# A GLA and convolution trunk on one core: v and output gate projected together, 512 columns wide, weights in three assigned places, layer 0's output projection block by block

## The chip, the cores and the metric

The kernel runs on one core of a Trainium2 chip. The metric is the device time of one execution, in microseconds; the time before is the median of three runs.

## What is computed

The input is 2048 tokens of 1024 channels in float32. Two residual layers follow each other, each ahead of its mixer with an RMSNorm, and a last RMSNorm ends it. The first layer (the kernel calls it layer 0) is gated linear attention with four heads; the second (layer 1) is a convolution module with a causal depthwise convolution of 31 taps, a layernorm and two gates. The change lies in the first:

```
proj = h @ w_in                      # q, k (512 each), v, z (1024 each), g_lr (16)
log_a = log_sigmoid(g_lr @ w_g2 + b_g) / 16
# per head (dk 128, dv 256), in chunks of 64 tokens:
b = cumsum(log_a);  q_dec = q*exp(b);  k_inv = k*exp(-b);  k_end = k*exp(b_last - b)
o = tril(q_dec @ k_inv.T) @ v + q_dec @ S;   S = exp(b_last)*S + k_end.T @ v
o = rmsnorm_per_head(o) * gn_w * silu(z)
x = x + o @ w_out
```

## The kernel before

Precision: every projection runs as three float32r matmuls, since each operand is split into a high part (`ah`, `wh`) and a low part (`al`, `wl`): high x high, high x low, low x high (`mm3`).

Weights: they come from HBM in units of 128 x 2048 values (1 MB). `load_unit` brings a unit in two halves through the staging tile `wr` (two of them); ScalarE casts each half to `wh`, GpSimd subtracts to get `wl` (VectorE for the first two units). Two places hold units; a place is free when TensorE's last matmul with it is done. `next_unit` keeps two units ahead, in the order of the list `order`.

Layer 0 works on half the tokens at a time (1024, two blocks of 512). `start_block` loads x, splits it (`prep_x`) and computes the low-rank gate (`gate_low`: sixteen matmuls with the gate weights `wgs`, a tile of its own) and E = exp(b). Then `head` runs four times: `qk` projects q and k feature-major, 128 columns of the weights against 512 tokens; `values` projects v for eight tiles of 128 tokens, token-major, 24 matmuls of 256 columns each; a loop over the same eight tiles then projects the gate z, again 24 matmuls of 256 columns, and issues the attention core in three stages, one tile apart: `scores`, `mix` and `turn`. v stays in eight pairs of tiles meanwhile. `out1` is the output projection: pairs of weight units, each pair against block 0 and then block 1. Its sum of squares for the next layer is added on GpSimd. After block 0 of the second pair it calls `ahead`, which prepares the next half's (or layer 1's) first block.

Layer 1 projects, convolves on VectorE, ScalarE and GpSimd beside it, normalises, and projects out. A scheduler places the instructions on each engine's in-order queue from a model of their times and from priorities; SP's queue issues all DMAs, also in order. PSUM has three banks `mm` for projections, two `pb` and three `pm`.

## Time and profile before

| what | us |
|---|---|
| median of the runs (1691.0 to 1695.15) | 1691.66 |
| span of the profiled execution | 1691.3 |
| TensorE busy in it | 1617.2 (96%) |
| VectorE busy | 1015.6 (60%) |
| GpSimd busy | 936.0 (55%) |
| ScalarE busy | 742.2 (44%) |
| layer 0, first half of the tokens | about 0 to 457 |
| layer 0, second half | about 457 to 858 |
| layer 1 | about 858 to 1691 |

Busy times are those of one profiled execution. Matmuls are pipelined, so a matmul's row is longer than the step from its start to the next one's; the steps are what adds up to time.

### The profile page before, as it was taken

Reading aid. Unit: us, or ns where it says so; the run is one execution under the profiler, and the core shown is the slowest. Engines: PE = TensorE matmul, PEld = TensorE weight load, DVE = VectorE, ACT = ScalarE, POOL = GpSimd, SP = SyncE. Lnnn points to the kernel's source line nnn. Section 1 sums busy time; section 2 is a strip of 40 time slices with the busy share of each in tenths; the row PEclk is TensorE's granted clock in tenths of the full one; section 3 lists DMA queues with packets and bytes.
Section 4 is the critical chain, followed back from the end, with each engine's and each line's share of the span. In section 5 each row is a group of like instructions: output and inputs, shape, how many; then the busy total and the mean of one; then the engine's idle time right before and its main releaser. Section 6 shows DMA issues by size and latency. Waiting matters only on the chain.

```text
span 1691.3 us, 23564 instructions
## 1 busy us (share of the span) xinstructions
PE 1617.2 (96%) x9028; PEld 1413.4 (84%) x9028; DVE 1015.6 (60%) x1473; ACT 742.2 (44%) x1254; POOL 936.0 (55%) x795
## 2 busy tenths in 40 slices
PE   8999999999999999999999999998999999997887
PEld 6989998988889999999888887876777778776687
DVE  7423232342334323226153999989799999987865
ACT  6645252343466444325232544544462554434432
POOL 4444343334745342424433999983788997465553
PEclk9999999999999999999999999999999999998998
DMA  5021111244511121204461111225127122632743
GB/s 188 30 78 57 63 51 57 76 130 139 164 34 55 58 72 42 75 33 132 132 196 46 63 50 57 85 80 154 38 69 238 61 68 94 206 125 88 235 176 124
DMA packets 74015, 165.68 MB, mean 98 GB/s; under 512 B 7760, under 2 KB 16464, under 8 KB 73904
## 3 DMA queue, kind: packets, MB, share of 16 engines
q1 hardware_dynamic: 73904, 164.19, 29.9%
q8 instruction: 70, 1.15, 0.3%
q14 instruction: 41, 0.34, 0.1%
HBM read 128.51 MB, written 35.65 MB: 97 GB/s over the span
## 4 chain that ended last, share of the span: by engine, by line
PE 62%; DVE 16%; POOL 7%; DMA 6%; issue 4%; ACT 3%; SPq 0%; POOLq 0%; DVEq 0%; ACTq 0%
PE mm L144 52%; DVE pb L638 6%; PE pb L144 3%; DVE al L190 2%; DMA wr<-in_wall_dram 2%; PE pb L388 1%; POOL wl L125 1%; PE pb L390 1%; POOL convB L624 1%; DVE S L713 1%; PE pm L379 1%; POOL convA L624 1%; DVE d L734 1%; POOL b L736 1%; DVE pb L642 1%
## 5 line engine op out<-in xcount | busy, mean ns | idle before, releaser
L144 PE MATMUL mm<-ah,wh 128*128 128x512 f32 (+1 forms) x1600 | 599.1, 389 | 43.2 <-DVE u L761 10.7
L144 PE MATMUL mm<-al,wh 128*128 128x512 f32 (+1 forms) x1600 | 594.6, 387 | 1.7 <-DVE al L190 1.7
L144 PE MATMUL mm<-ah,wl 128*128 128x512 f32 (+1 forms) x1600 | 592.9, 387 | 2.3 <-POOL wl L125 2.3
L125 POOL TENSOR_TENSOR wl<-wr,wh 128x1024 fp32r<-128x1024 f32 x140 | 358.5, 2575 | 195.2 <-ACT wh L124 190.3
L144 PEld LDWEIGHTS mm<-ah,wh 128*128 128x128 f32 x1600 | 304.0, 191 | 109.0 <-DVE u L761 13.1
L144 PEld LDWEIGHTS mm<-ah,wl 128*128 128x128 f32 x1600 | 303.3, 191 | 62.4 <-POOL wl L125 4.2
L144 PEld LDWEIGHTS mm<-al,wh 128*128 128x128 f32 x1600 | 303.9, 191 | 59.7 <-DVE al L190 2.6
L144 PE MATMUL mm<-wh,ah 128*128 128x256 f32 x896 | 259.2, 289 | 0.0
L144 PE MATMUL mm<-wh,al 128*128 128x256 f32 x896 | 254.6, 284 | 0.0
L144 PE MATMUL mm<-wl,ah 128*128 128x256 f32 x896 | 254.2, 284 | 0.0
L124 ACT ACTIVATE wh<-wr 128x1024 fp32r<-128x1024 f32 x144 | 145.3, 1050 | 109.0 <-PE mm L144 78.9
L638 DVE SCALAR_TENSOR_TENSOR pb<-u,C,pb 128x512 f32<-128x512 f32 x252 | 183.8, 747 | 0.5
L638 DVE SCALAR_TENSOR_TENSOR pb<-u,dwc,pb 128x512 f32<-128x512 f32 x240 | 179.4, 748 | 1.6
L144 PEld LDWEIGHTS mm<-wl,ah 128*128 128x128 f32 x896 | 171.4, 191 | 0.4
L144 PEld LDWEIGHTS mm<-wh,ah 128*128 128x128 f32 x896 | 171.3, 191 | 0.4
L144 PEld LDWEIGHTS mm<-wh,al 128*128 128x128 f32 x896 | 171.3, 191 | 0.0
L622 ACT ACTIVATE prod<-u,C 128x512 f32<-128x512 f32 x148 | 105.6, 721 | 137.6 <-POOL convA L624 78.5
L624 POOL TENSOR_TENSOR convA<-convA,prod 128x512 f32<-128x512 f32 x74 | 99.5, 1344 | 6.6 <-ACT prod L622 3.0
L624 POOL TENSOR_TENSOR convB<-convB,prod 128x512 f32<-128x512 f32 x74 | 99.6, 1346 | 3.9 <-ACT convB L620 0.7
L397 DVE SCALAR_TENSOR_TENSOR S<-S,dec,pb 128x256 f32<-128x256 f32 x56 | 26.8, 479 | 95.4 <-PE pb L144 95.3
L401 POOL TENSOR_TENSOR ss<-ss,e 128x1 f32<-128x1 f32 x64 | 13.3, 208 | 124.5 <-ACT g L400 124.5
L523 DVE TENSOR_TENSOR Q<-mm,Q 128x512 f32<-128x512 f32 x32 | 22.0, 688 | 92.7 <-PE mm L144 78.9
(205 smaller groups left out, 2245.3 us busy)
## 6 DMA issues: line engine op xcount, KB each, us to landing
wr<-in_wall_dram SPq DMA_DIRECT2D x144, 512.0 KB, 4.1
raw<-in_xT_dram SPq DMA_DIRECT2D x32, 256.0 KB, 3.8
Q<-in_xT_dram SPq DMA_DIRECT2D x32, 256.0 KB, 3.2
x_scratch<-Q SPq DMA_DIRECT2D x32, 256.0 KB, 3.2
sz_scratch<-t SPq DMA_DIRECT2D x32, 256.0 KB, 2.3
b<-sz_scratch SPq DMA_DIRECT2D x32, 256.0 KB, 3.8
g_scratch<-st SPq DMA_DIRECT2D x48, 128.0 KB, 1.9
raw<-g_scratch SPq DMA_DIRECT2D x24, 256.0 KB, 3.7
```

The costliest lines, as they stand in the source:

```text
L124: act.activation(wh[:, ks, :], raw, AF.Copy)
L125: (dve if i < 2 else pool).tensor_tensor(wl[:, ks, :], raw, wh[:, ks, :].bitcast(F32), ALU.subtract)
L144: pe.matmul(ps, s, m, start=(i == 0), stop=(i == 3 * n - 1))
L190: dve.tensor_tensor(lo, src, hi.bitcast(F32), ALU.subtract)
L379: pe.matmul(s_ps[:, 0:192], ki[:, js], Q[:, j].rearrange("p s c -> p (s c)"), start=True, stop=True)
L388: pe.matmul(o_ps, Q[:, j, 0:2].rearrange("p s c -> p (s c)"), S[h], start=True, stop=False)
L390: pe.matmul(o_ps, x, y, start=first and n == 0, stop=n == 2)
L397: dve.scalar_tensor_tensor(S[h], S[h], dec[:, j:j + 1], kv, ALU.mult, ALU.add)
L523: dve.tensor_tensor(xr, ps, xr, ALU.add)
L622: act.activation(p, src, AF.Copy, scale=w)
L624: pool.tensor_tensor(acc, acc, p, ALU.add)
L638: dve.scalar_tensor_tensor(dstm, src, w, ps, ALU.mult, ALU.add)
```

## The change

The weights of a head's v and gate are packed side by side, 512 columns wide, and come as two units, each with half of the 1024 input channels. `values` now projects both in 24 matmuls of 512 columns into one bank, takes v from its first half and the gate from its second, and the core's stages run in the same loop. The units have three places, assigned by hand in `order`: place 2 lies in a pool of layer 0 alone. `out1` runs block 0 with all four units and then block 1 with all four, so that its units are loaded twice; `ahead` is called between the blocks. The gate weights lose their own tile: they are built once in a staging tile `wr`, written to HBM, and read back into a `wr` for each of the three later blocks. Head 0 takes block 0's q and k, four token tiles, then starts block 1. `raw` has four buffers where it had five, `vh` and `vl` three where they had eight.

```
-    wp = ctx.enter_context(tc.tile_pool(name="wp", bufs=2))
+    wp = ctx.enter_context(tc.tile_pool(name="wp", bufs=1))
...
-    order = list(range(0, 16)) * 2
+    half = [(3 * h + j, (2, 0, 1)[j]) for h in range(HEADS) for j in range(3)]
+    half[1:3] = [(1, 1), (2, 0)]
+    half += [(12 + j, c) for j, c in enumerate((2, 0, 1, 2))]
+    half += [(12 + j, c) for j, c in enumerate((0, 2, 1, 0))]
+    order = half * 2
+    units = []
     for sched in SCHED:
...
+    order += [(u, (n + 1) % 2) for n, u in enumerate(units)]
...
+        wpool = wq if place == 2 else wp
+        wh = wpool.tile([P, UW], F32R, name=f"wh{place}")
+        wl = wpool.tile([P, UW], F32R, name=f"wl{place}")
...
+    def prefetch(n):
+
+        while len(wstate["ready"]) < n and wstate["next"] < len(order):
+            if order[wstate["next"]][1] in [u[1] for u in wstate["ready"]]:
+                return
+            load_unit()
...
+    def next_wide(expect, ahead):
+
+        prefetch(ahead)
+        w = []
+        for s in range(2):
+            hl = [t.rearrange("p (k c) -> p k c", c=2 * DV) for t in pop_unit(expect + s)]
+            w += [(hl[0][:, k], hl[1][:, k]) for k in range(KT // 2)]
+        return w
...
+    def gate_weights(first):
+
+        t = wp.tile([P, UW // 2], F32R, name="wr", bufs=2)
+        wgs = t.rearrange("p (k c) -> p k c", c=P)
+        if not first:
+            sp.dma_start(out=t.bitcast(F32), in_=wgd)
+            return wgs
...
+    def values(hf, i, w, a_b):
+
+        ps = mm_bank()
+        proj_t(ps, w, a_b, i % 4)
+        q = hf * 8 + i
+        vh, vl = (l1p.tile([P, DV], F32R, name=n, bufs=3) for n in ("vh", "vl"))
+        act.activation(vh, ps[:, 0:DV], AF.Copy, scale=r2[:, q:q + 1])
+        dve.scalar_tensor_tensor(vl, ps[:, 0:DV], r2[:, q:q + 1], vh.bitcast(F32), ALU.mult, ALU.subtract)
+        sz = l1p.tile([P, DV], F32, name="sz", bufs=3)
+        act.activation(sz, ps[:, DV:2 * DV], AF.Silu, scale=rt[:, q:q + 1])
+        return (vh, vl), sz
...
+        w = next_unit(base, 3)
+        if h == 0:
+            qkb.append(qk(h, w, a[0], EEs[0]))
+            wv = next_wide(base + 1, 2)
+            for i in range(4):
+                tokens(i, wv)
+            start_block(hf, 1, a, EEs, g3s)
+            qkb.append(qk(h, w, a[1], EEs[1]))
+            prefetch(1)
+        else:
+            for b in range(2):
+                run_late(1 if b == 0 else 0)
+                qkb.append(qk(h, w, a[b], EEs[b]))
+            wv = next_wide(base + 1, 3)
+            for i in range(4):
+                tokens(i, wv)
+        if h < HEADS - 1:
+            nxt = gate(h + 1, g3s)
+        for i in range(4, 8):
+            tokens(i, wv)
...
-        for pair in range(2):
-            ws = [next_unit(12 + 2 * pair), next_unit(13 + 2 * pair)]
-            for b in range(2):
+        for b in range(2):
+            t0 = hf * TH + b * NB
+            acc = l1p.tile([P, NB], F32, name="acc", bufs=2)
+            for u in range(4):
+                w = next_unit(12 + u, 3)
```

The scheduler's queues show what this does to the order. SP's queue near the program's start; `raw` are tiles of x, `wr` are staging tiles, `wr_126` holds the gate weights. Before:

```order
L123 DMA wr_170<-in_wall_dram 128x1024
L269 DMA raw_176<-in_xT_dram 128x512
L123 DMA wr_201<-in_wall_dram 128x1024 [waits DMAHW0_49]
L247 DMA ident_84<-in_ident_dram 128x128 [waits DMAHW1_49]
L269 DMA raw_185<-in_xT_dram 128x512 [waits DMAHW2_49,DVE_49,Activation_49]
L249 DMA tmp_215<-in_wg2_dram 96x512 [waits DMAHW3_49]
L269 DMA raw_194<-in_xT_dram 128x512 [waits DMAHW4_49,DVE_49,Pool_49]
```

and now:

```order
L133 DMA wr_175<-in_wall_dram 128x1024
L279 DMA wg_scratch_115<-wr_126 128x1024 [waits DVE_49]
L283 DMA ident_84<-in_ident_dram 128x128 [waits DMAHW0_49]
L285 DMA tmp_220<-in_wg2_dram 96x512 [waits DMAHW1_49]
L305 DMA raw_181<-in_xT_dram 128x512 [waits DMAHW2_49,DVE_49,Activation_49]
L286 DMA masks_116<-in_masks_dram 128x192 [waits DMAHW3_49]
L305 DMA raw_190<-in_xT_dram 128x512 [waits DMAHW4_49,DVE_49,Pool_49]
L305 DMA raw_199<-in_xT_dram 128x512 [waits DMAHW5_49,DVE_49,Activation_49]
L305 DMA raw_212<-in_xT_dram 128x512 [waits DMAHW6_49,DVE_49,Pool_49]
L133 DMA wr_206<-in_wall_dram 128x1024 [waits DMAHW7_49,DVE_49]
```

The second half of unit 0 (`wr_201`, now `wr_206`) stood two rows behind the first and now stands nine rows behind it, with a wait for VectorE.

TensorE's queue where the first token tile is projected, behind block 0's q and k. Before, v alone (`wh_275` is its unit; `pm_241` is a sum of squares):

```order
L144 MATMUL pb_365<-wh_275,ah_136 128x256 [waits Activation_49]
L144 MATMUL pb_394<-wh_275,ah_136 128x256
L144 MATMUL pb_365<-wl_276,ah_136 128x256 [waits DVE_49]
L144 MATMUL pb_365<-wh_275,al_137 128x256
L144 MATMUL pb_365<-wh_275,ah_143 128x256
L144 MATMUL pb_365<-wl_276,ah_143 128x256
L144 MATMUL pb_365<-wh_275,al_144 128x256
L166 MATMUL pm_241<-ones_85,acc_135 128x1 [waits DVE_49]
L166 MATMUL pm_241<-ones_85,acc_135 128x1 x3
L144 MATMUL pb_365<-wh_275,ah_152 128x256
```

and now the second half of the channels of v and gate (`wh0_290`, the second unit; `pm_267` is the gate), and the first row of the second token tile:

```order
L172 MATMUL mm_370<-wh0_290,ah_179 128x512 [waits Activation_49]
L172 MATMUL mm_370<-wl0_291,ah_179 128x512 [waits Pool_49]
L172 MATMUL mm_370<-wh0_290,al_180 128x512
L172 MATMUL mm_370<-wh0_290,ah_188 128x512
L172 MATMUL mm_370<-wl0_291,ah_188 128x512
L172 MATMUL mm_370<-wh0_290,al_189 128x512
L346 MATMUL pm_267<-g3_264,g2t_114 128x512 [waits DVE_49,PE_49]
L172 MATMUL mm_370<-wh0_290,ah_197 128x512 [waits Activation_49]
L172 MATMUL mm_370<-wl0_291,ah_197 128x512 [waits Pool_49]
```

Four rows that wait for casts or GpSimd's splits of the second unit now stand inside the first token tile's group.

TensorE's queue in the output projection of the first half, where the next half's sixteen gate matmuls stand. Before, in the last quarter (`mm_4533` is a projection of block 1 with the third unit), ten of the sixteen, each with a wait, and the other six some 40 rows later:

```order
L144 MATMUL mm_4533<-ah_3923,wh_3965 128x512
L166 MATMUL pm_4376<-ones_85,acc_3953 128x1 [waits PE_49,Pool_49]
L288 MATMUL pm_4447<-ah_4384,wgs_111 128x512 [waits Activation_49]
L288 MATMUL pm_4447<-al_4385,wgs_111 128x512 [waits DVE_49]
L288 MATMUL pm_4447<-ah_4391,wgs_111 128x512 [waits Activation_49]
L288 MATMUL pm_4447<-al_4392,wgs_111 128x512 [waits DVE_49]
L288 MATMUL pm_4447<-ah_4399,wgs_111 128x512 [waits Activation_49]
```

and now, in block 1's second unit, with the first nine behind one wait:

```order
L172 MATMUL mm_3676<-ah_3112,wh2_3582 128x512 [waits DVE_49,Activation_49]
L172 MATMUL mm_3676<-al_3113,wh2_3582 128x512
L193 MATMUL pm_3456<-ones_85,acc_3160 128x1 [waits PE_49,Pool_49]
L324 MATMUL pm_3529<-ah_3464,wr_3527 128x512 [waits DMAHW3_49,PE_49]
L324 MATMUL pm_3529<-al_3465,wr_3527 128x512
L324 MATMUL pm_3529<-ah_3471,wr_3527 128x512
L324 MATMUL pm_3529<-al_3472,wr_3527 128x512
L324 MATMUL pm_3529<-ah_3479,wr_3527 128x512
```

The gate matmuls moved from the third and fourth unit's part to the second's, and read their weights from a staging tile that was loaded for them.

## Rows read from the trace of the kernel before

**Rows 1.** The page's parts 1 and 2: busy us per engine; granted clock, 40 slices.
```profile
PE 1617.2 (96%) x9028; PEld 1413.4 (84%) x9028; DVE 1015.6 (60%) x1473; ACT 742.2 (44%) x1254; POOL 936.0 (55%) x795
PEclk9999999999999999999999999999999999998998
```
**Rows 2.** Chain of waits: start us, length us, what; matmuls without a gap, counted.
```profile
144.25 14.39 PE mm L144 x120
...
372.81 56.49 PE mm L144 x249
```
**Rows 3.** Waits of TensorE: us in total, times, longest; layer 0, then layer 1.
```profile
PE pm L310 <- DVE g L302: 1.4, 1, 1.4
PE pb L144 <- DVE vl L438: 1.3, 1, 1.3
...
PE mm L144 <- DVE Q L332: 1.0, 1, 1.0
...
PE mm L144 <- DVE u L761: 10.7, 5, 3.2
PE mm L144 <- DVE u L845: 7.5, 5, 2.3
```
**Rows 4.** Stretches: us, busy us (instructions) of each engine, clock, DMA share, GB/s.
```profile
142.00:225.00 83.00, 83.00 (x591) 78.46 (x591) 24.95 (x52) 34.21 (x70) 30.24 (x40) 1.00 0.18 58
...
372.00:457.00 85.00, 85.00 (x381) 70.51 (x380) 24.86 (x29) 31.04 (x48) 46.61 (x29) 1.00 0.49 150
0.00:27.54 27.54, 19.17 (x65) 14.28 (x66) 21.89 (x28) 19.62 (x31) 9.66 (x21) 1.00 0.80 251
...
858.00:1691.00 833.00, 772.49 (x3540) 638.02 (x3538) 712.29 (x922) 361.20 (x524) 583.81 (x390) 0.97 0.34 112
```
**Rows 5.** Groups by line and form: count, busy us, mean ns, idle before.
```profile
L144 PE MATMUL mm<-wh,ah 128*128 128x256 f32 x896 | 259.2, 289 | 0.0
...
L144 PE MATMUL pb<-wh,ah 128*128 128x256 f32 x128 | 37.4, 294 | 1.3 <-DVE vl L438 1.3
...
L438 DVE SCALAR_TENSOR_TENSOR vl<-mm,r,vh 128x256 fp32r<-128x256 f32 x48 | 22.9, 483 | 89.3 <-ACT vh L437 89.2
...
L437 ACT ACTIVATE vh<-mm,r 128x256 fp32r<-128x256 f32 x48 | 22.1, 469 | 55.2 <-PE mm L144 55.2
...
L318 ACT ACT_TABLE_LOAD x10 | 12.8, 1283 | 0.2
```
**Rows 6.** Timelines of the start: SP (DMA issue), VectorE, TensorE; start us, length us.
```profile
3.55 0.44 SPq L123 DMA_DIRECT2D wr<-in_wall_dram  x1
...
4.50 0.67 SPq L123 DMA_DIRECT2D wr<-in_wall_dram  x1
...
12.50 1.21 DVE L125 TENSOR_TENSOR wl<-wr,wh 128x1024 fp32r<-128x1024 f32 x1
...
25.27 0.39 PE L288 MATMUL pm<-al,wgs 128*128 128x512 f32 x1
...
27.54 0.40 PE L144 MATMUL pb<-wh,ah 128*128 128x256 f32 x2
...
48.43 0.50 PE L144 MATMUL mm<-ah,wh 128*128 128x512 f32 x1 [0.95 <-DVE Q L332]
```
**Rows 7.** What staging costs: landing (whole run; first 60 us), cast (mean ns), GpSimd's splits.
```profile
wr<-in_wall_dram SPq DMA_DIRECT2D x144, 512.0 KB, 4.1
...
wr<-in_wall_dram SPq DMA_DIRECT2D x8, 512.0 KB, 4.8
...
L124 ACT ACTIVATE wh<-wr 128x1024 fp32r<-128x1024 f32 x144 | 145.3, 1050 | 109.0 <-PE mm L144 78.9
...
400.78 4.75 POOL L125 TENSOR_TENSOR wl<-wr,wh 128x1024 fp32r<-128x1024 f32 x2 [3.44 <-ACT wh L124]
```
**Rows 8.** TensorE's timeline where the second half starts, and that stretch's clock (after the busy times).
```profile
469.60 0.39 PE L144 MATMUL mm<-ah,wh 128*128 128x512 f32 x1
471.26 0.39 PE L144 MATMUL pb<-wh,ah 128*128 128x256 f32 x1 [1.27 <-DVE vl L438]
...
472.19 0.28 PE L144 MATMUL pb<-wl,ah 128*128 128x256 f32 x1
473.84 0.47 PE L310 MATMUL pm<-g,g2t 96*128 96x512 f32 x1 [1.37 <-DVE g L302]
...
474.20:481.00 6.80, 6.80 (x34) 6.80 (x33) 1.93 (x5) 6.02 (x7) 3.20 (x3) 0.50 0.00 1
```

More of the change, by code (lines that the diff above doesn't have):

```diff
@@ L103 @@
              U[:3] + Z[:1] + U[3:6] + Z[1:2] + U[6:] + Z[2:]]
[L104 removed]
+    half = [(3 * h + j, (2, 0, 1)[j]) for h in range(HEADS) for j in range(3)]
[4 more added lines that the diff above has]
+    units = []
     for sched in SCHED:
[L106 to L107 removed]
+        units += [16 + j if s == "u" else 24 + j for s, j in sched]
+    units += list(range(28, 32)) * 4
+    order += [(u, (n + 1) % 2) for n, u in enumerate(units)]
     wstate = {"next": 0, "ready": []}
```

120 lines of the change are left out of this document (41 added, 79 removed).

## The prediction

> **What bounds the kernel now.** The page's first part says TensorE is busy 96% of the span, and its granted clock stands at 2.4 GHz in nearly every slice [rows 1]. A busy matmul row proves little, because the matmuls overlap, so the next view is the timeline of starts: from one start to the next is what a matmul really costs. The chain of waits gives the same number in one row, pieces of uninterrupted matmuls with their count [rows 2]. The 128x256 projections run at 14.39/120 = 0.1199 us each, the 128x512 ones at 56.49/249 = 0.2269 us. Two narrow ones take 0.2398 us for the columns of one wide one, so each matmul carries 0.0129 us that doesn't depend on its width. In layer 0 TensorE hardly waits: its longest waits after the program's start are 1.0 to 1.4 us [rows 3]. Time taken off its matmuls there therefore comes off the run, unless a new wait takes its place. Layer 1 (858 to 1691 us) is different: VectorE is busy 712 of 833 us [rows 4] and TensorE waits for it again and again [rows 3].
>
> **The part that must pay: width.** Per half, head and token tile the v and gate projections were 24 + 24 matmuls of 256 columns; now they are 24 of 512. Over 2 halves, 4 heads and 8 tiles, 3072 narrow ones go (2688 into mm and 384 into pb, from three forms of 896 and three of 128 [rows 5]) and 1536 wide ones come: 1536 x (0.2398 - 0.2269) = **-19.8 us**. All of it lies on TensorE's path. The row for the wide form was taken with the weights as stationary side; with the tokens there, as now, the trace has only narrow ones. I take the wide row, because its form is the nearest in columns, and the rival D below is the other bound.
>
> The Trainium skill, page "TensorE: Matmul & The Clock Gate", section "Back-to-back issue gap", gives the isolated gap of a matmul at full clock as N/2.4 + 2.5 ns. That is 109.2 and 215.8 ns, so a pair would save only 2.6 ns and all 1536 about 4 us (an estimate from that page); the sum below would end near 1694. Both rows are 11 ns above the formula, so the measurement decides.
>
> **The start.** This is where the change puts a wait back. The gate weights no longer have a tile of their own: they sit in one of the two staging tiles (wr) through which all weights pass, until the sixteen gate matmuls are done. And head 0 now needs both units of v and gate directly after block 0's q and k, where before it needed v alone.
> - Before, both halves of unit 0 were issued at 3.55 and 4.50 us [rows 6]. Now the second half waits until VectorE has split the first, at 12.50 + 1.21 = 13.7 us; with the landing of 4.1 to 4.8 us, the cast of 1.05 and the split of 1.21 [rows 6, 7] it is ready near 20. TensorE comes to it at about 21, so this costs under 1 us, and q and k end near 28.4 where it was 27.54 [rows 6].
> - First half of v|gate: its staging tile is free at 20, so it is ready near 27 to 28. It meets TensorE.
> - Second half: it waits for the tile that holds the gate weights (last gate matmul before at 25.27 [rows 6], a little earlier now since the order puts it before the second half of q) and is ready near 30; TensorE is there at 30.
> - Third and fourth quarter (unit 2): each waits for the split of the quarter two before it. 28 + 4.8 + 1.05, and then GpSimd's 2.4 (4.75 for two [rows 7]), gives 36.4; TensorE wants it at 31.6: **4.8 us**. The fourth follows at about 40 (its issue stands behind x loads in SP's queue): **2.5 us** more.
> - The second v|gate tile needs a PSUM bank. Three exist, q and k hold two until the gate's E is there (before, TensorE waited until 48.43 for VectorE to read q [rows 6]), so it waits until VectorE and ScalarE have emptied the first: 0.47 + 0.48 + a table load of 1.28 + 0.47 [rows 5, 7] = **2.7 us**.
> Together 10.0, with the first bullet's 0.9 some 11; the wait of 1.0 before 48.43 goes: **+10 us**. From below: with landings of 3 us and nothing queued between the steps, four quarters come some 7 us earlier, so +3. From above: two pauses of 1.4 to 1.6 us were enough at 470 us to lower the clock for 6.8 us [rows 8], a loss of 3.4, and one late x tile more: +15.
>
> **The second half's start.** Before, the next half's x was prepared only when three quarters of the output projection were through, since each pair of weights served both blocks. TensorE then stood 1.4 us (469.60 to 471.26, less a pitch) and 1.5 us (472.19 to 473.84), and after that the granted clock was 0.5 for 6.8 us [rows 8], half of which is lost: 3.0 + 3.4 = 6.4 us. Block by block, the first block's operand tiles come free after 8 instead of 12 of the projection's 16 groups of 24 x 0.2269 = 5.45 us, so preparation starts some 22 us earlier, and TensorE's queue has the gate group in the second unit of block 1, where before it stood in the last quarter, cut in pieces. I take **-5**; bounds -6.4 and +2 (the group's last rows wait for x tiles whose loads stand behind a weight half in SP's queue, and GpSimd, which splits weights and adds squares in turn, is the slower hand).
>
> **Added work that should hide.** The output weights are loaded once per block: 8 units more, 8 MB, 16 casts x 1.05 = 16.8 us of ScalarE and 16 splits x 2.4 = 38 us of GpSimd. In the output stage GpSimd is busy 46.6 of 85 us [rows 4]; 19 more leaves it under 80%. A unit now serves 2 x 24 x 0.2269 = 10.9 us, and its two splits take 4.75. The gate stage in the middle of a head adds 14 table loads x 1.28 = 18 us to a ScalarE that is 41% busy in a head (34.2 of 83 us [rows 4]). At the six turns to heads 1 to 3 the two v|gate units can be cast only after the last token tile of the head before. Four quarters through two staging tiles: 1.05 + 2.4 for the first, and the third after its landing, 3.5 + 4.1 + 1.05 + 2.4 = 11, the fourth 13.5 us; q and k of the new head take 4 x 24 x 0.2269 = 21.8 us. 8 us of cover are left for what else GpSimd does there. Layer 1 keeps its program; on VectorE some 25 of the layernorm's and convolution's rows stand earlier or later by a few places. I put **+1** for all of this, between -3 and +5.
>
> **Sum.** The profiled execution spans 1691.3 us, 0.4 below the median of 1691.66, so the sum is made from the median: 1691.7 - 19.8 + 10 - 5 + 1 = **1678**.
>
> **Rivals.**
> - A, the start is cheap: landings as short as 3 us, +3 there, second half -6.4: 1691.7 - 19.8 + 3 - 6.4 = 1668.5. For it: transfers at the start ran at 251 GB/s and more [rows 4]. Against: the four quarters are a chain of waits, not a rate. Chance 0.2.
> - B, the gain is spent: the clock falls at the start (+15) and the second half gains nothing: 1691.7 - 19.8 + 15 + 2 = 1689. Chance 0.15.
> - C, slower: the v|gate weights come late at every head's turn. Place: the first v|gate row of heads 1 to 3, both halves, where TensorE would wait for GpSimd's split. Price: 6 us for each us past the cover of 21.8; it decides from 2.3 us late (13.7 us, the whole gain). With 5 us late: 1678 + 30 = 1708. For it: GpSimd's queue is in order and holds splits that wait for casts that wait for TensorE. Against: 8 us of slack. Chance 0.07.
> - D, the change doesn't do what it says: with tokens as the stationary side a wide matmul takes as long as two narrow ones (0.2398): 1691.7 + 10 - 5 + 1 = 1698. Against: the columns are the same work and both pitches fit one fixed part and a part per column. The skill's formula above lies between this and the forecast. Chance 0.05.
>
> **How the numbers follow.** Forecast 0.53, from 1671 to 1687; A 0.2, B 0.15, C 0.07, D 0.05. A measurement here can tell about 0.3% (5 us) from no change: faster means below 1686.6, slower above 1696.7. Forecast less its upper edge (0.03) and A give faster 0.70; that edge, B and 0.01 of the rest give same 0.19; most of C and D give slower 0.11. The range leaves out C, D and the lower edge of A: 1667 to 1692.
>
> **What would show it.** Right: wide mm rows of layer 0 at 0.227 from start to start; 1536 of them; TensorE waiting at 28 to 45 us for wh, wl and sz, about 10 us in all; no stop near the second half's start and no clock of 0.5 there; layer 1 as long as before, 833 us. Wrong: a pitch near 0.24 (D); waits for wl at each head's first tile (C); layer 1 longer or shorter by more than 5 us, which no step here accounts for.

## The result

| | median us | ratio to before, 95% interval |
|---|---|---|
| before | 1693.4 | |
| changed | 1719.98 | 1.0167, 1.0136 to 1.0198 |

The change makes the kernel 1.7% slower; the forecast was 1678 with a range to 1692. The profiled execution of the changed kernel takes 1716.06 us and spans 1714.1 us, 22.8 more than before. Its page, in parts 1, 2 and 5 (answers to [rows 1, 2, 5]):

```profile
PE 1617.4 (94%) x7492; PEld 1337.6 (78%) x7492; DVE 1035.0 (60%) x1473; ACT 775.4 (45%) x1284; POOL 980.4 (57%) x811
...
PEclk9899999999999999999999999999999999998999
...
L172 PE MATMUL mm<-wh,ah 128*128 128x512 f32 x512 | 206.9, 404 | 10.2 <-ACT sz L475 6.0
```

The 1536 wide matmuls are there (three forms of 512), and TensorE has 1536 matmuls fewer. The new figure is the last one: the wide group stood idle for 10.2 us, 6.0 of it behind ScalarE's `sz`, a wait that did not exist. Where the time went is read from the timeline of TensorE: the start of the first q matmul of each head, of the first output matmul, and of layer 1's 300th, 900th and 1500th projection matmul gives the length of each stage, all in one profiled execution of either kernel.

| stage, on TensorE | before us | changed us | difference | forecast |
|---|---|---|---|---|
| first half: head 0, from its first q | 90.9 | 107.4 | +16.5 | +7.5 |
| first half: heads 1 to 3 | 249.7 | 247.5 | -2.2 | -7.4 |
| first half's output projection, second half's head 0 | 187.7 | 187.0 | -0.7 | -7.5 |
| second half: heads 1 to 3 | 250.8 | 251.6 | +0.8 | -7.4 |
| second half's output projection | 91.7 | 92.6 | +0.9 | 0 |
| layer 1: first 300 matmuls | 71.3 | 77.8 | +6.5 | 0 |
| layer 1: 300th to 900th | 139.7 | 141.1 | +1.4 | 0 |
| layer 1: 900th to 1500th | 162.6 | 167.6 | +5.0 | 0 |
| layer 1: the rest | 421.4 | 416.9 | -4.5 | 0 |

The forecast column shares the -19.8 out at 2.5 a head; its +1 for hidden work had no place. The same starts correct the stage bounds that stand ahead of the prediction: before, TensorE begins the second half at 447.7 us and layer 1 at 883.1 us, not at 457 and 858.

**The width itself came nearly as forecast.** In a head, 384 narrow matmuls took 46.8 to 47.3 us from start to start; the 192 wide ones take 44.3 to 45.1. That is 2.3 us a head, 18 over eight heads instead of 19.8. The step is indeed 0.227 [rows 2], but not everywhere. TensorE's timeline in head 2:

```profile
272.28 0.48 PE L172 MATMUL mm<-wh,ah 128*128 128x512 f32 x1
272.59 0.40 PE L172 MATMUL mm<-wl,ah 128*128 128x512 f32 x1
272.83 0.39 PE L172 MATMUL mm<-wh,al 128*128 128x512 f32 x1
273.06 0.39 PE L172 MATMUL mm<-wh,ah 128*128 128x512 f32 x1
273.28 0.39 PE L172 MATMUL mm<-wl,ah 128*128 128x512 f32 x1
```

The first step of a group, behind the small matmuls of the core, is 0.31 us, the next two 0.24 and 0.23, then 0.22 to 0.23. The row that priced the term [rows 2] came from the output projection, where nothing small stands between.

**At the start TensorE stops, then runs at half speed.** Stretches of the start (us, busy times by engine, granted clock, DMA share, GB/s), and TensorE's timeline in them, the answer to [rows 6]:

```profile
30.00:35.00 5.00, 3.08 (x11) 1.91 (x11) 4.70 (x5) 3.40 (x5) 3.91 (x3) 1.00 0.74 203
35.00:40.00 5.00, 2.69 (x6) 1.68 (x6) 3.91 (x3) 4.27 (x7) 4.47 (x3) 0.69 0.54 194
40.00:45.00 5.00, 3.83 (x8) 2.00 (x7) 3.48 (x2) 2.11 (x5) 3.90 (x2) 0.50 0.38 128
45.00:50.00 5.00, 1.14 (x3) 0.95 (x4) 2.45 (x2) 4.94 (x6) 2.49 (x2) 0.50 0.03 11
50.00:55.00 5.00, 5.00 (x15) 3.92 (x14) 1.99 (x4) 1.37 (x3) 2.10 (x4) 0.60 0.00 0
```
```profile
35.38 0.49 PE L172 MATMUL mm<-wh,ah 128*128 128x512 f32 x1 [0.75 <-ACT wh L134]
37.80 0.79 PE L172 MATMUL mm<-wl,ah 128*128 128x512 f32 x1 [1.93 <-POOL wl L135]
...
43.71 0.63 PE L172 MATMUL mm<-wl,ah 128*128 128x512 f32 x1
44.13 0.63 PE L172 MATMUL mm<-wh,al 128*128 128x512 f32 x1
48.87 0.79 PE L172 MATMUL mm<-wh,ah 128*128 128x512 f32 x1 [4.10 <-ACT sz L475]
```

A stop is what a step from start to start takes beyond the matmul's usual step. Stops of over 0.4 us come to 15.4 us in head 0, where before had 3.8: 1.3 at its first matmul (before 1.6), 6.6 between 29 and 42 us for `wl` and `wh`, 4.5 for `sz`, 3.0 at 96 and 103 us for `sz` again and for block 1's q, whose bank VectorE empties once E is there. The clock is 0.50 between 37 and 54 us; there 17 matmuls step by 0.43 instead of 0.23 (43.71 to 44.13), which is 3.3 us. What ScalarE does in the longest stop:

```profile
44.09 0.63 ACT L352 ACTIVATE tmp<-tmp 128x512 f32<-128x512 f32 x1
44.74 1.28 ACT L354 ACT_TABLE_LOAD   x1
46.03 0.63 ACT L354 ACTIVATE tmp<-tmp 128x512 f32<-128x512 f32 x1
46.57 0.46 ACT L472 ACTIVATE vh<-mm,r 128x256 fp32r<-128x256 f32 x1
47.04 1.28 ACT L475 ACT_TABLE_LOAD   x1
48.34 0.47 ACT L475 ACTIVATE sz<-mm,rt 128x256 f32<-128x256 f32 x1
```

The first token tile's matmuls were over at 44.5. Its bank is free only at 48.8, since ScalarE's queue has the gate's Exp, a table load and Ln ahead of v, and a second load ahead of Silu. The Trainium skill, page "ScalarE: Activation LUTs", section "What ACT_TABLE_LOAD costs", gives 1283 ns for the load and some 1380 more for a drain; here Exp ends at 44.72 and Ln starts at 46.03, so the switch takes 1.31 us and no more.

**The stop at the second half's start moved, it didn't go** (answer to [rows 8]). TensorE, then VectorE:

```profile
449.13 0.39 PE L172 MATMUL mm<-ah,wh 128*128 128x512 f32 x1
452.82 0.47 PE L346 MATMUL pm<-g,g2t 96*128 96x512 f32 x1 [3.30 <-DVE g L338]
...
453.78 0.63 PE L172 MATMUL mm<-ah,wh 128*128 128x512 f32 x1
454.21 0.63 PE L172 MATMUL mm<-al,wh 128*128 128x512 f32 x1
...
450.26 2.41 DVE L338 TENSOR_TENSOR g<-tmp,g 32x512 fp32r<-32x512 f32 x1 [3.95 <-ACT g L337]
```

The gate matmul now stands in the middle of block 1's projection, and the last 60 matmuls of that projection stand behind it in TensorE's in-order queue while it waits for `g`; the next 12 read a weight unit that was in use already. The clock follows: eight steps of 0.43, 1.6 us lost. Further on, the second half's head 0 has the same two stops at block 1 as the first half's, 1.1 us for `sz` and 1.9 for q's bank.

**Inside the heads there are new waits.** Counted here as a step's length beyond 0.24 us, whatever the matmul's width, stops of over 0.1 us in heads 1 to 3 came to 0.4 us in either half before; now to 3.9 and 5.7. The longest waits of the second half (us in total, times, longest); GpSimd and VectorE at one of them (576 us), ScalarE at the longest (628 us):

```profile
PE pb L172 <- DVE g L439: 2.4, 2, 1.6
PE pb L426 <- POOL stl L419: 0.6, 1, 0.6
```
```profile
568.79 2.40 POOL L135 TENSOR_TENSOR wl<-wr,wh 128x1024 fp32r<-128x1024 f32 x1 [2.00 <-ACT wh L134]
571.53 2.41 POOL L135 TENSOR_TENSOR wl<-wr,wh 128x1024 fp32r<-128x1024 f32 x1 [0.34 <-ACT wh L134]
573.89 0.19 POOL L437 TENSOR_TENSOR ss<-ss,e 128x1 f32<-128x1 f32 x1
...
575.19 0.54 POOL L438 TENSOR_TENSOR ss<-ss,mhalf 128x1 f32<-128x1 f32 x1
...
575.77 0.48 DVE L439 SCALAR_TENSOR_TENSOR g<-pb,ss,sz 128x256 f32<-128x256 f32 x1 [5.37 <-POOL ss L438]
```
```profile
622.81 1.28 ACT L475 ACT_TABLE_LOAD   x1
...
624.60 1.28 ACT L358 ACT_TABLE_LOAD   x1
...
626.43 0.37 ACT L436 ACTIVATE g<-pb 128x256 f32<-128x256 f32 x1
```

A 0.19 us step on 128 numbers, whose input ScalarE had ready at 571.8, stands behind a weight split until 573.9, and its second part behind two other steps until 575.2; VectorE's `g` waits for it, and a `pb` bank for `g`. At 626.43 it is ScalarE's square for the same step that comes behind two table loads.

All steps of heads 1 to 3 in both halves, sorted by the matmul that begins them, show what became of the saving. The steps of the v and gate matmuls (with 147 narrow ones of the core that share their line) fell from 300.2 to 287.1 us, 13.1 saved. The steps that begin with one of the core's small matmuls grew from 65.6 to 74.5, and those that begin with q or k from 134.6 to 137.9: 12.2 lost.

**Layer 1 starts without its data.** SP's queue, VectorE and TensorE's wait at the passage (layer 1's first matmul is at 898.0):

```profile
899.47 2.84 SPq L225 DMA_DIRECT2D raw<-x_scratch  x4
...
906.27 2.09 DVE L226 SCALAR_TENSOR_TENSOR raw<-raw,C,E 128x512 f32<-128x512 f32 x3 [4.88 <-DMA raw<-x_scratch]
...
PE mm L172 <- ACT ah L216: 3.9, 1, 3.9
```

These are block 1's first x tiles. Their data is not what is late: block 1's first four channels were stored by 882.6 and had landed at 889.3. The loads stand in SP's in-order queue behind the block's residual loads and stores, up to the store of its seventh channel. That store went out at 898.96, and the loads 1.5 us after layer 1 had begun; before, the store went out at 881.42 and the loads at 881.90, 1.2 us ahead of it. After the wait of 3.9 us the clock falls too (0.83 between 900 and 920 us).

### The profile page after: what moved, and what is told of

It reads as the page before. It is cut to its first block, busy times and chain, and to the rows that moved or that the text cites. A ratio compares the mean times of both kernels' runs of the same rounds, so it can differ in the third digit from the quotient of the medians.

```text
span 1714.1 us, 20604 instructions
## 1 busy us (share of the span) xinstructions
PE 1617.4 (94%) x7492; PEld 1337.6 (78%) x7492; DVE 1035.0 (60%) x1473; ACT 775.4 (45%) x1284; POOL 980.4 (57%) x811
## 4 chain that ended last, share of the span: by engine, by line
PE 48%; DVE 26%; DMA 9%; POOL 6%; issue 5%; ACT 5%; SPq 0%; POOLq 0%; DVEq 0%; ACTq 0%
PE mm L172 41%; DVE pb L671 12%; DMA wr<-in_wall_dram 5%; POOL wl L135 2%; DVE al L217 2%; DVE pb L675 2%; DVE d L767 1%; PE pb L424 1%; ACT wh L134 1%; PE pb L426 1%; PE pb L172 1%; DVE S L746 1%; PE pm L415 1%; DVE u L794 1%; DMA b<-sz_scratch 1%
## 5 line engine op out<-in xcount | busy, mean ns | idle before, releaser
L135 POOL TENSOR_TENSOR wl<-wr,wh 128x1024 fp32r<-128x1024 f32 x156 | 393.6, 2534 | 200.7 <-ACT wh L134 193.5
L172 PEld LDWEIGHTS mm<-ah,wh 128*128 128x128 f32 x1600 | 305.7, 192 | 113.6 <-ACT t L807 13.4
L172 PE MATMUL mm<-wh,ah 128*128 128x512 f32 x512 | 206.9, 404 | 10.2 <-ACT sz L475 6.0
L172 PE MATMUL mm<-wl,ah 128*128 128x512 f32 x512 | 203.3, 397 | 4.7 <-POOL wl L135 2.9
L172 PE MATMUL mm<-wh,al 128*128 128x512 f32 x512 | 203.6, 398 | 0.0
L172 PEld LDWEIGHTS mm<-wh,ah 128*128 128x128 f32 x512 | 97.3, 190 | 31.2 <-ACT sz L475 7.1
L419 POOL TENSOR_TENSOR stl<-sT,sth 128x128 fp32r<-128x128 f32 x64 | 32.5, 509 | 150.4 <-ACT sth L418 150.4
L172 PEld LDWEIGHTS mm<-wl,ah 128*128 128x128 f32 x512 | 97.3, 190 | 24.8 <-POOL wl L135 3.9
L172 PEld LDWEIGHTS mm<-wh,al 128*128 128x128 f32 x512 | 97.3, 190 | 19.9
L472 ACT ACTIVATE vh<-mm,r 128x256 fp32r<-128x256 f32 x64 | 30.2, 472 | 121.4 <-PE mm L172 121.3
L473 DVE SCALAR_TENSOR_TENSOR vl<-mm,r,vh 128x256 fp32r<-128x256 f32 x64 | 30.9, 484 | 84.9 <-ACT vh L472 83.8
```

The lines of the kernel that those rows point to most:

```text
L135: (dve if i < 2 else pool).tensor_tensor(wl[:, cs], raw, wh[:, cs].bitcast(F32), ALU.subtract)
L172: pe.matmul(ps, s, m, start=(i == 0), stop=(i == 3 * n - 1))
L419: pool.tensor_tensor(stl, st, sth.bitcast(F32), ALU.subtract)
L472: act.activation(vh, ps[:, 0:DV], AF.Copy, scale=r2[:, q:q + 1])
L473: dve.scalar_tensor_tensor(vl, ps[:, 0:DV], r2[:, q:q + 1], vh.bitcast(F32), ALU.mult, ALU.subtract)
```

## The experiments

Medians, with the ratio to before on the same chip; the last three of the first column left work out and are single executions.

| run | median us | ratio, 95% interval |
|---|---|---|
| e1_narrow | 1740.76 | 1.0287, 1.0266 to 1.0309 |
| e2_own_tile | 1731.05 | 1.0206, 1.0157 to 1.0256 |
| e3_stl_dve | 1727.11 | 1.0209, 1.0188 to 1.0229 |
| e4_pairs | 1721.66 | 1.0177, 1.0151 to 1.0202 |
| e5_block_alone | 1713.02 | 1.0131, 1.0101 to 1.0160 |
| e6_own_pb | 1730.22 | 1.0236, 1.0203 to 1.0269 |
| e7_split_dve | 1722.50 | 1.0179, 1.0142 to 1.0216 |
| e8_gate_early | 1726.01 | 1.0210, 1.0177 to 1.0243 |
| e9_pairs_second | 1712.90 | 1.0133, 1.0116 to 1.0150 |
| e13_wide_heads13 | 1712.06 | 1.0142, 1.0109 to 1.0175 |
| e14_own_always | 1727.51 | 1.0210, 1.0182 to 1.0238 |
| e15_wide_own | 1701.55 | 1.0061, 1.0041 to 1.0081 |
| e16_own_pairs2 | 1721.19 | 1.0171, 1.0143 to 1.0200 |
| e10_no_tables | 1705.79 | |
| e11_no_start_weights | 1716.40 | |
| e12_neither | 1701.42 | |

### Is the width worth anything?

e1_narrow takes the width alone back:

```
-        mm3(ps, [(a[k][0][:, s], a[k][1][:, s], w[k][0], w[k][1]) for k in range(KT)])
+        for c in range(2):
+            cs = slice(c * DV, (c + 1) * DV)
+            mm3(ps[:, cs], [(..., w[k][0][:, cs], w[k][1][:, cs]) for k in range(KT)])
```

> The changed kernel with one edit: each token tile's v and gate are again two groups of 24 matmuls of 256 columns, into the two halves of one PSUM tile; loads, places, order of stages and output projection stay as changed. Theory (the width pays): in heads 1 to 3 of the changed kernel 192 wide matmuls take 44.3 to 45.1 us from start to start where the 384 narrow ones before took 46.8 to 47.3, so 2.3 us a head and 18 us over 8 heads come back: layer 0 ends near 916 us instead of 898, the run near 1738. Rival (a wide matmul costs two narrow ones, and 2.3 us is only where other work falls between them): the run stays within 4 us of the changed kernel's 1716 to 1724. Layer 1 is not edited; if its length depends on the order that the scheduler gives it, it may differ by some us from 755 in any of these kernels, so the sums are made at the end of layer 0.

Measured: layer 1 starts at 920.1 instead of 898.0, so the width is worth 22 us in this kernel, and the rival (one wide matmul costs two narrow ones) falls. But not 2.3 us a head: heads 1 to 3 get longer by 4.2 and 1.2 us only, the rest sits mostly at the two starts. In those heads the narrow kernel stops for 1.3 us in each half where the wide one stops for 3.9 and 5.7. The heads narrow but in the new order, v, gate and core in one loop, take 504.5 us and before 500.5, and their steps that begin with the core's small matmuls 71.8, which is 6.2 of the 8.9 that the changed kernel loses there: this points to the order of the steps more than to the width. But these lengths move between kernels. In the thirteen with wide heads 1 to 3 and the gate's tables, the changed kernel among them, the heads of both halves take 497.6 to 506.7 us; with narrow ones 499.1 (e5_block_alone) to 504.5. The 13.8 us that the matmuls save show in none of them.

### What makes the start late?

e2_own_tile moves the first gate weights out of the staging tiles; e6_own_pb adds two PSUM banks to it; e14_own_always keeps the gate weights out of the staging tiles in all four blocks:

```
-        t = wp.tile([P, UW // 2], F32R, name="wr", bufs=2)
+        ts = [s2.tile([P, NB], F32R, name="st", bufs=BUFS["st"]) for _ in range(2)]
...
-        ps = mm_bank()
+        ps = b_bank() if hf == h == 0 and i in (1, 2) else mm_bank()
```

> The changed kernel with one edit: at the first start the gate weights are split into two tiles of the ring st (idle until head 0 turns its outputs) instead of one of the two staging tiles wr; all else as changed. Theory (the start's loss comes mainly from the shared staging tile, which delays the second half of unit 0 from 4.5 to 13.6 us and the first quarter of v and gate from 13.8 to 22.5 us): stops before 50 us shrink from 14 us to about 5, the half-speed clock between 37 and 54 us goes, head 1 of the first half starts near 109 us instead of 119.3, the run near 1709. Rival (four quarters in a row through two staging tiles and three PSUM banks bind, whoever uses them first): head 1 starts at 116 or later and the half-speed stretch stays; the run within 4 us of the changed kernel.

> The changed kernel with two edits at the first start: gate weights in tiles of their own (as in the run that did this alone) and the second and third v|gate token tiles written to the two pb banks that are idle there, so that TensorE doesn't stand until ScalarE has emptied the only free mm bank. Theory (with the staging tile out of the way the start is bound by PSUM tiles that wait for the token factors of GpSimd and the table loads of ScalarE: stops of 5.0 and 6.1 us before a third and a fourth token tile): these two stops shrink to 3 us together or less, no or a short half-speed stretch before 60 us, head 1 of the first half starts at 109 to 113 us instead of 122.5 (own tiles alone) and 119.3 (changed); the run 1706 to 1712, if the rest is as in the changed kernel. Rival (the serial chain of weight quarters or the token factors themselves bind, whatever the banks): head 1 starts at 118 or later.

> The changed kernel with one edit: the gate weights never pass through the staging tiles wr; they lie in two tiles of the ring st for both blocks of the first half, and are loaded there again once for the second half. The earlier run had taken them out of wr for the first block alone. Theory (what the sharing costs is the reloads for block 1 and for the second half, which stand in the SP queue ahead of weight quarters): the first half's head 0 takes 98 to 103 us (changed 107.4, first block alone 110.0), and from the first half's projection to head 1 of the second half 181 to 184 us instead of 186.7. Rival (PSUM tiles, tables and the gate's chain bind at the start, so that no way of staging helps): head 0 stays at 106 or more, the other stretch within 2 us.

Measured: head 0 takes 110.0, 117.1 and 108.7 us, against 107.4 changed. All three theories fall. In e2_own_tile the weights came earlier, and TensorE ran through to 32.7 us, but then stood 2.3 us for `wl` and 5.0 and 6.1 us for `sz`. TensorE's waits from 28 us on in e14_own_always show the same:

```profile
PE mm L172 <- ACT sz L477: 12.7, 4, 5.9
PE mm L172 <- POOL wl L135: 3.4, 2, 2.4
```

With two more banks (e6_own_pb) it stood 5.2 us for `sz` at a later tile, ran on and then stood 8.8 us for `Q`: E came at 61 us, since the gate's matmul stood in the queue behind three token tiles, where the changed kernel has it inside the first. Moving one obstacle brings out the next.

e10_no_tables replaces the gate's Exp and Ln by copies, e11_no_start_weights lets the first head read unit 0 for its v and gate, e12_neither does both:

```
-            act.activation(ab, ab, AF.Ln, bias=1.0)
+            act.activation(ab, ab, AF.Copy)
...
-    order = half * 2
+    order = half[:1] + half[3:] + half
...
+                wv = [(f[0][:, k % 4], f[1][:, k % 4]) for k in range(KT)]
```

> The changed kernel with the gate's four Exp and Ln steps in layer 0 replaced by copies of the same size, which leaves their function out (the output is not the reference's) and with it the switching of ScalarE's tables between them and Silu. Theory (ScalarE's table loads of 1.28 us between Silu and the gate's functions are what makes squares, casts and PSUM tiles late): the gate stage in the middle of a head costs nothing then: heads 1 and 2 of both halves, 337.8 us together in the changed kernel, 4 to 8 us shorter; the first head, 107.4 us, 4 to 6 us shorter (stop of 4.5 us at 44 us). Rival (the waits come from GpSimd's queue and from weights): heads 1 and 2 within 2 us, the first head within 2 us.

> The changed kernel without the loading and splitting of the first head's two v|gate units in the first half: its wide matmuls read unit 0 instead (so v and gate of that head are not the reference's), and never wait for weights of their own. Theory (the start is lost to the arrival of the v|gate quarters, stops of 6.6 us between 29 and 42 us and the half-speed clock that they bring): head 1 starts at 106 to 109 us instead of 119.3. Rival (the gate's chain from the sums over x to E, which frees the PSUM tiles of q and k, and block 1's x tiles set the start, and weights only fill the time until then): head 1 starts at 114 or later.

> Both edits of the two runs before together: no gate tables in layer 0 and no v|gate weights to load for the first head. Theory (weights and tables are the two halves of the start's loss): head 1 starts at 100 to 104 us, before any stop of over 2 us after 28 us. Rival (block 1's x tiles, whose preparation now stands behind four token tiles on ScalarE and VectorE, bind in any case): head 1 still at 110 or later, with stops before 50 or between 95 and 106 us.

Measured: head 0 takes 103.7, 100.4 and 96.6 us. Tables are worth 3.7 us there, weights 7.0 (half of which head 1 gives back: it takes 88.4 instead of 84.4), both 10.8. The tables fall just short of their 4 us, and of the other two neither theory nor rival has its number: head 1 starts at 111.9 and 109.0. The longest wait that is left in e12_neither is the gate's chain to `g`:

```profile
PE pm L346 <- DVE g L338: 4.7, 1, 4.7
```

And e10_no_tables tells of the heads: heads 1 and 2 of both halves take 330.3 us instead of 337.8, as its theory said, and e12_neither 332.8 instead of e11_no_start_weights' 340.2; in e10_no_tables the stops in heads 1 to 3 fall to 2.2 and 1.4. In the other kernels with wide heads and the tables left in, these heads take 336.1 to 345.4 us, so both are outside the spread. ScalarE's table loads in layer 0, changed and then without the gate's functions:

```profile
L475 ACT ACT_TABLE_LOAD x15 | 19.2, 1283 | 0.3
L354 ACT ACT_TABLE_LOAD x14 | 18.0, 1283 | 0.2
L358 ACT ACT_TABLE_LOAD x14 | 18.0, 1283 | 0.2
L352 ACT ACT_TABLE_LOAD x10 | 12.8, 1283 | 0.2
```
```profile
L276 ACT ACT_TABLE_LOAD x1 | 1.3, 1283 | 0.7 <-PEq L971 0.7
L475 ACT ACT_TABLE_LOAD x1 | 1.3, 1283 | 0.0
```

### Can the waits in the heads be moved away?

e3_stl_dve gives `stl` to VectorE, e7_split_dve all weight splits of layer 0, e8_gate_early puts the gate stage ahead of the token tiles:

```
-            pool.tensor_tensor(stl, st, sth.bitcast(F32), ALU.subtract)
+            dve.tensor_tensor(stl, st, sth.bitcast(F32), ALU.subtract)
...
-            (dve if i < 2 else pool).tensor_tensor(wl[:, cs], raw, ...)
+            (dve if i < len(half) * 2 else pool).tensor_tensor(wl[:, cs], raw, ...)
...
             wv = next_wide(base + 1, 3)
+            if h < HEADS - 1:
+                nxt = gate(h + 1, g3s)
             for i in range(4):
                 tokens(i, wv)
-        if h < HEADS - 1:
+        if h == 0:
             nxt = gate(h + 1, g3s)
```

> The changed kernel with one edit: the small remainder of the scores (stl, 128x128) is taken by VectorE instead of GpSimd. Theory (the new waits inside heads 1 to 3, 3.9 us in the first half and 5.7 in the second where before had 0.4, come from GpSimd, whose weight splits of 2.4 us each stand ahead of stl in its queue): these waits fall by half or more, heads 1 to 3 of both halves together get 4 to 6 us shorter, the run near 1714. Rival (they come from the order on TensorE's own queue and from PSUM tiles): heads stay within 1 us.

> The changed kernel with one edit: all weight remainders (wl) of layer 0 are taken by VectorE (1.2 us each) instead of GpSimd (2.4 us). Theory (part of the new waits in heads 1 to 3 comes from GpSimd's queue: at 568.8 to 573.9 us two splits stand ahead of the sum of squares ss that VectorE, and through it a PSUM tile, needs): the stops behind stl and ss go, heads 1 to 3 of both halves together 3 to 6 us shorter than the changed kernel's 499.1 us; the stop of 1.75 us behind the gate's table loads stays. Rival (VectorE's queue then makes the same kind of wait, since splits stand ahead of its S and vl): heads within 1.5 us or longer.

> The changed kernel with one edit: in heads 1 and 2 the next head's gate (Exp and Ln with their table loads) is issued before the first v|gate token tile, as it stood before, and not between the fourth and the fifth. Theory (in the middle of the tiles its tables alternate with Silu's, and ScalarE comes late to the squares that GpSimd, VectorE and a PSUM tile wait for: the stop of 1.75 us at 626 us): table loads fall by 8 to 14, the stops at the end of heads 1 and 2 go, those heads together 2 to 4 us shorter. Rival (only the place of the wait moves; ScalarE is 30 to 40% busy and has the time anyway): heads within 1 us.

Measured: heads 1 to 3 of both halves take 502.0, 506.7 and 503.3 us, against 499.1 changed and 500.5 before; in e8_gate_early the table loads fall from 54 to 50 only. All three theories fall: no edit makes the heads shorter, and the wait comes back on VectorE's queue (`S`, `g`) or, in e8_gate_early, on `sth`, as the rivals of e7_split_dve and e8_gate_early said. The 1 us that two of the rivals allowed is exceeded (e3_stl_dve 2.9, heads 1 and 2 of e8_gate_early 1.3), but heads 1 to 3 of the first half take 247.4 to 253.0 us in kernels that are edited elsewhere (e9_pairs_second, e2_own_tile), so lengths of 2 or 3 us tell nothing here.

### What does the block order do?

e4_pairs puts the whole projection back to pairs, e5_block_alone gives the kernel before the block order and nothing else, e9_pairs_second goes by pairs in the second half only, e16_own_pairs2 joins that with e14_own_always:

```
-        for b in range(2):
...
-            for u in range(4):
-                w = next_unit(12 + u, 3)
...
+        for pair in range(2):
+            ws = [next_unit(12 + 2 * pair, 3), next_unit(13 + 2 * pair, 3)]
+            for b in range(2):
```

> The changed kernel with one edit: layer 0's output projection goes by pairs of weight units for both blocks again, each unit loaded once; v and gate stay wide, the start stays as changed. Theory (the block-by-block order only moved the stop at the second half's start to the other side of the boundary: 3.5 us at 449 us and a half-speed clock of 3.4 us instead of two stops of 1.4 and 1.5 us and 6.8 us at half speed): from the first half's output projection to head 1 of the second half the time stays within 3 us of the changed kernel's 187.0 us (before: 187.7). Rival (block by block is worth the 5 us that the prediction gave it, and something else in that stage lost them): this stretch gets 5 us longer or more. Layer 1: if its length hangs on the scheduler's order and not on any work of the change, it differs between these four kernels by several us around 755 (before: 746); if it hangs on the weight places or the later start, it is 755 within 2 in all four.

> The kernel before with one edit, the third part of the change alone: layer 0's output projection goes block by block, its weights loaded once per block; v and gate stay narrow, places, start and heads as before. Theory (block by block costs rather than gains: what it saves at the second half's start is lost inside the projection, and at the passage to layer 1 the x tiles of the first block come late, since their loads stand behind the second block's residual loads in the SP queue: 6.4 us on the first 300 matmuls of layer 1 in the changed kernel, 0 where the projection went by pairs): second half's start within 4 us of before, first 300 matmuls of layer 1 at 77 to 78 us instead of 71.3, the run 6 to 10 us over before. Rival (the block order gives the 5 us of the prediction, and what was lost at both places belongs to the wide heads): run 3 to 7 us under before, the first 300 matmuls at 71 to 72 us. Layer 1 keeps the order of before here, so the stretch from its 900th to its 1500th matmul should take 163 us, as before, and not the 168 to 171 of the changed kernels.

> The changed kernel with one edit: the output projection of the second half alone goes by pairs for both blocks again; the first half's stays block by block. Theory (each order is right at one place: block by block lets the wide head 0 of the second half start, where pairs cost 13.9 us more between the first half's projection and the second half's head 1; but at the passage to layer 1 it puts the x loads behind residual loads, which costs 5.5 to 7.1 us on layer 1's first 300 matmuls in every kernel that has it, 0.3 in the one that doesn't): layer 0 as in the changed kernel (first layer-1 matmul at 896 to 900 us), layer 1's first 300 matmuls 71 to 72 us instead of 77.8, the run 1709 to 1713 in its profile. Rival (the 6 us follow from where layer 1's first weights and tiles lie, not from the projection's order): first 300 matmuls at 77 us or more.

> The changed kernel with the two edits that its losses point to: gate weights never in the staging tiles, and the second half's output projection by pairs. Theory (their gains add): what the first edit gives in layer 0 (0 to 8 us), and layer 1's first 300 matmuls in 71 us instead of 77.8: the run 1700 to 1711 in its profile, still slower than before. Rival (with the gate weights apart the two don't add, because the second half's start was bound elsewhere): 1709 or more.

Measured, from the first half's projection to the end of the second half's head 0: 199.2 us with pairs, against 187.0; so with the wide head 0 the block order is worth 12 us there, and e4_pairs' rival was right. In the kernel before it costs 8.2 us there (195.9 against 187.7) and 8.0 in the second half's projection, 20 us in all: the rival of e5_block_alone falls; its theory had the passage right but allowed 4 us at the second half's start and 10 in all. Layer 1's first 300 matmuls take 70.8 to 74.8 us in the five runs that go by pairs in the second half, and 74.6 to 78.8 in the others. The two that meet differ in kind: e15_wide_own's 74.8 has a wait of 2.2 us for `Q` and a lower clock, e10_no_tables' 74.6 the wait of 3.6 us for block 1's x but no lower clock. In e9_pairs_second SP and VectorE read

```profile
893.90 3.98 SPq L226 DMA_DIRECT2D raw<-x_scratch  x4
...
899.88 2.08 DVE L227 SCALAR_TENSOR_TENSOR raw<-raw,C,E 128x512 f32<-128x512 f32 x3 [2.35 <-DMA raw<-x_scratch]
```

2.3 us ahead of its first layer-1 matmul at 896.2; TensorE has no wait there, and the profiled execution takes 1707.7, a little under the 1709 to 1713 expected. The order taken out (e4_pairs, e9_pairs_second) and put in alone (e5_block_alone) give the same: that settles the 6.5 us. e16_own_pairs2 does not reach the sum: layer 1's first 300 matmuls take 72.5 us, but head 0 takes 110.4, no better than e14_own_always' 108.7, and the profiled execution 1724.65, which is the rival's side.

### The width by itself

e13_wide_heads13 has v and gate wide in heads 1 to 3 only. Head 0 has v first and narrow, stored in the third place, and the projection goes by pairs. e15_wide_own also keeps the gate weights out of the staging tiles in all blocks.

```
+        if h == 0:
...
+            store = [wq.tile([P, UW], F32R, name=n) for n in ("wh2", "wl2")]
+            vs = [[t[:, i * DV:(i + 1) * DV] for t in store] for i in range(8)]
```

> The first part of the change by itself, where it needs no new start: v and gate wide in heads 1 to 3 of both halves, while head 0 has them narrow, v for all eight tiles first and the gate behind, as before, and the output projection goes by pairs, as before; the gate weights are in tiles of their own at the first start. Theory (the matmuls of a head get 2.3 us shorter, 13.8 over six heads, but the wide heads spend most of that on waits, since v, gate and the score steps of a tile now reach ScalarE and GpSimd together; and the start and the passages cost nothing when they are as before): head 1 of the first half starts at 102 to 105 us, heads 1 to 3 of the two halves take 247 to 249 and 250 to 253 us (before 249.7 and 250.9), layer 1 starts at 879 to 885 us and, with the scheduler's other order, takes 795 to 800 us: the run 1688 to 1697. Rival (the waits in the heads of the changed kernel follow from its late start and its block-by-block projection, and the width is free without these): heads 1 to 3 take 242 to 245 us in each half, layer 1 starts near 870 us, the run 1676 to 1684.

> The run before this one (wide in heads 1 to 3 only, head 0 and projection as before) with the gate weights never in the staging tiles. There head 0 took 103.2 us instead of 90.9, and the SP queue stood 25.3 us before the reload of the gate weights, with the quarters of the gate unit behind it. Theory (that reload alone made the start late): head 0 takes 90 to 94 us, heads 1 to 3 of the first half 246 to 249 us, layer 1 starts at 883 to 891 us, the run 1692 to 1702. Rival (the smaller ring of x tiles, 4 instead of 5, or the new places make it late): head 0 stays at 99 or more.

Measured: head 0 takes 103.2 and 91.3 us (before 90.9). In the first, SP's queue stood before the reload of the gate weights, with the gate unit's quarters behind it:

```profile
SPq L268 <- POOL wl L134: 25.3, 1, 25.3
```

So sharing the staging tiles does cost 12 us, but only where nothing else makes the start late; in e14_own_always, with 12.7 us of waits for `sz`, it gave nothing. The rival of e15_wide_own, the ring of four x tiles, falls with it. Heads 1 to 3 take 249.3 and 248.3 us in e15_wide_own (before 249.7 and 250.8): of 13.8 us that their matmuls save, 2.9 arrive. The theory of e13_wide_heads13 held on the heads (249.4 and 250.8 us) and not on its start; that of e15_wide_own held to within 0.3 us on the heads, and its median is inside the range. e15_wide_own is the fastest of the changed kernels and still 0.6% slower than before: the second half's start costs 6.1 us, and layer 1 8.7 (803.7 against 795.0 to its last matmul). No run here beats the kernel before. The shorter rings of `vh` and `vl`, three tiles where there were eight, were not tried apart.

## Why the prediction was wrong

By stage, the forecast missed by 13.4 us in heads 1 to 3 of the two halves, 9.0 in the first half's head 0, 8.4 in layer 1, 6.8 at the second half's start and 0.9 in its output projection.

- **Width, -19.8.** The rate was nearly right: 18 us in the matmuls, rival D refuted. The step that failed is "Time taken off its matmuls there therefore comes off the run". It was meant to hold "unless a new wait takes its place", and in heads 1 to 3 that happened: 13.1 us saved, 12.2 lost in the steps that begin with the core's small matmuls and with q and k. Before, v was there for all eight tiles when the score steps began; now v's cast and Silu stand in each tile's chain. That the gain is spent in the heads shows in thirteen kernels (497.6 to 506.7 us against 500.5), and that the table loads are part of the price in e10_no_tables (491.6). What the order of the steps and what each other step of the chain costs is not shown apart: moving single steps to another engine or place only moved the wait. By an estimate from the Trainium skill's formula (page "TensorE: Matmul & The Clock Gate", section "Back-to-back issue gap") a pair would have saved 2.6 ns; from the 2.3 us a head it is 12 ns.
- **Start, +10 (bounds +3 to +15).** Measured 16.5 + 2.3 for the width = +18.8. The place and its waits were right: the weights' stops were 6.6 us where the steps gave 8.2 (the third quarter's sum is 36.2, not 36.4), and `sz` 4.5 where they gave 2.7. What the sum lacked is what follows a stop: the half-speed clock, 3.3 us, which stood in the upper bound as 3.4 and not in the value, and the 3.0 us at block 1, which appeared nowhere. Stops (15.4 less 3.8) and clock make 14.9 of the 18.8; the other 3.9 lie in smaller steps. Taken away alone, tables are worth 3.7 and weights 7.0; 8 us (96.6 + 2.3 - 90.9) stay without either, 4.7 of it the gate's chain. The rest is not shown apart.
- **Second half's start, -5 (bounds -6.4 to +2).** Measured -0.7 + 2.3 = +1.6. Both old stops and their half-speed clock went, as forecast, but the step "TensorE's queue has the gate group in the second unit of block 1" was read as a gain: from there the gate's next matmul, in the third unit, stops a queue that had work. The two stops and the clock of before give 6.4 us back; the gate's stop (3.5 from start to start), its half-speed clock (1.6) and the 3.0 at block 1 take 8.1, which makes +1.7.
- **Hidden work, +1 (bounds -3 to +5).** What didn't hide is part of the 12.2 us above, not a second loss. The 14 more table loads (12 were measured: 54 against 42) were set against ScalarE's mean load of 41%. With 52 of the 54 gone, e10_no_tables is 7.5 us shorter in four heads; this is the price of all of them, those of before too, and what the 12 cost alone no run shows. A mean says nothing of the queue at the moment when a bank waits. No wait for `wl` at the heads' turns appeared: rival C's mechanism did not occur.
- **Layer 1, 0.** Two things were missed. The block order makes block 1's x late at the passage, +6.5 (e9_pairs_second, e5_block_alone). And the scheduler's order of layer 1 differs more than was said: 86 of VectorE's last 660 places hold another instruction, not some 25. It is the same in the fifteen runs that build on the changed kernel, and there the stretch from the 900th to the 1500th matmul takes 167.4 to 171.0 us; with the order of before it is 162.6 and 163.7 (e5_block_alone). The rest of layer 1 takes 414.1 to 420.3 against 421.4 and 418.2. So with this order go about 5 us more at one place and some less at the next. That the order is the cause is not shown: the same fifteen kernels also share the new weight places and the ring of four x tiles. Why the scheduler orders it otherwise, no run shows.
- **Sign.** Rival B (1689) had the right mechanisms, a lower clock and nothing gained at the second half, but as the far edge of two terms; that they came with new waits in the heads and at the passage is what made the kernel slower.

## What to carry to other kernels

A faster matmul is worth what the engines around it can follow: before counting its gain, follow one tile's chain through the other queues, step by step, and compare it with the tile's new time on TensorE. Where the faster matmul needs another order of the steps, price that order by itself, with the old matmuls in it. A stop costs more than itself (the clock after it, the ready work behind it in the queue), so the sum takes the clock wherever a row shows that stops of that length lowered it. And a loop order is judged at both ends: what the next stage needs first, and when this order finishes that.

## What the runs showed that was not expected

- The same layer 1, with the same order on VectorE, took 794 to 809 us to its last matmul in kernels that differ in layer 0 alone; some of that is the passage (70.8 to 78.8); why what follows it takes 723 to 731 was not followed. Differences of 5 us between kernels say little of a cause without a view of the stage.
- VectorE's `g` step of 32x512 took 2.41 us at 450 us beside two GpSimd splits, and 1.66 at 38 us; such lengths moved by a factor of 1.5 within one run.
